# A transformer block on one core: part of the first modulation row moved to VectorE, ScalarE and GpSimd, four early loads into rooms of later tiles, and the last norm's rows left in PSUM

## Chip, core and metric

The kernel runs on one core of one Trainium2 chip. The metric is device time in microseconds (us); the median of three runs of the kernel before is 1842.34 us (1841.93 to 1842.74).

## What is computed

One block on 256 tokens of width 2048, in float32. A condition vector `c` gives six modulation rows of 2048 (shift, scale and gate, for each half of the block); the first half mixes tokens by windowed attention and by a gated delta rule, the second is a mixture of 32 experts, of which each token takes two:

```python
mod = (silu(c) @ w_ada + b_ada)[:, None, :]            # 2048 x 12288
sh1, sc1, g1, sh2, sc2, g2 = split(mod, 6)
u = layer_norm(x) * (1 + sc1) + sh1
mix = token_mixer(u, w_in, ...)                         # u @ w_in, attention, delta rule, w_out
x = layer_norm(ALPHA * x + g1 * mix, ln1_g, ln1_b)
u = layer_norm(x) * (1 + sc2) + sh2
ffn = hier_moe(u, ..., w_gate_up, w_down)
x = layer_norm(ALPHA * x + g2 * ffn, ln2_g, ln2_b)      # the result
```

The change touches the way `sh1` is summed, the loads of the weights of `sh1` and `sc1`, a small constant, and the last `layer_norm`.

## The kernel before

Weights come from HBM in tiles of 128x2048 floats (1024 KB). `wload` (L75) takes a buffer from a pool of four and issues the load on SyncE's queue (SP), which works in order: a load whose buffer is still in use holds every load behind it.

`first_mods` (L157) makes `sc1` (`i` = 1) and `sh1` (`i` = 0) in four quarters `q` of 512 columns. For each it loads four tiles and multiplies every one with the replicated silu of `c` on TensorE (L179; a float32 matmul shows as two records, so a tile is eight). ScalarE copies the sum out of PSUM (L186); `use` (L159) sums the four groups of partitions by four small matmuls (L163, eight records) and adds the bias (L164). After the shift of a quarter, `use` also modulates the quarter's four blocks of the normalised, transposed input: VectorE scales and shifts (L168), ScalarE casts to the high part `uh` (L169), VectorE makes the low part `ul` (L170). `use` runs one tile late: the last shift of a quarter is summed after the first tile of the next quarter's scale. `first_mods` is a generator and gives way after each tile.

The first projection is split by the same quarters. `quarter` (L299) lists ten jobs per quarter: half a weight tile is split into a high part on ScalarE (`wh`, L262) and a low part on VectorE (`wl`, L263), with two buffers for `wl`, and multiplied by three matmuls per block (L267 to L269, `wq`). The sum is copied out by ScalarE in the first quarter (L321) and added by VectorE in the others (L323). `run` (L332) goes through the jobs and, four times per job, adds `per / 4` to a counter and takes a step of the given generator when it reaches 1: this writes the order of the work out by hand. Nine steps of `first_mods` come before the jobs; then each of the first three quarters takes up to eight steps of the next quarter's modulation at `QCH` = 0.73 per job (L754).

Later `ada_steps` (L198) makes the other four modulation rows: VectorE multiplies and adds tile by tile (L207), beside the rest of the projections. `gates` (L367) uses a small selection matrix `sel`, reduced from the identity (L378).

The experts run in 16 pairs: `gate_up` (L1166) multiplies 16 tiles, `turned` (L1185) transposes, `down` (L1202) multiplies eight tiles in four column blocks and adds to the residual (L1225 to L1230). Their loads go round `rings` of 17 buffers: four of `wload`, six and seven of two other pools (L1239); the last loads avoid the four of `wload` (L1250), since `last_rows` (L1350) places the gain and bias of the last norm there, each in a tile of 128x2048: TensorE spreads a row over the partitions (L152) into PSUM and ScalarE copies it (L1355), in the last pair. After a branch for overfull experts, the last norm runs on VectorE: `ln_affine` (L126) makes two passes over each of five pieces, which are then written out (L1397 to L1399).

## Time and profile before

| what | before |
|---|---|
| median of three runs | 1842.34 us (1841.93 to 1842.74) |
| the profiled execution | 1841.24 us |
| its span, first to last instruction | 1839.4 us |
| TensorE busy | 1746.7 us, 95% of the span |
| VectorE busy | 904.7 us, 49% |
| ScalarE busy | 516.3 us, 28% |
| GpSimd busy | 42.0 us, 2% |
| HBM traffic | 624.64 MB read, 341 GB/s over the span |
| mean granted TensorE clock | 0.985 |

Busy shares are means over stages with different limits, so a stage is read by itself: its busy times, its DMA rate, and which wait ends last. TensorE's busy time contains matmuls whose ends are modelled. A row of a timeline that stands for several instructions (`x8`) gives the time from the first's start to the last's end.

### The profile page before, as it was taken

The page shows a single profiled execution, that of the slowest core. Times are in us where ns is not written, and L with a number is a line of the kernel's source. Part 1 is how long each engine was busy: PE and PEld are TensorE (multiplying, and loading weights), DVE is VectorE, ACT ScalarE, POOL GpSimd, SP SyncE. Part 2 cuts the span into 40 slices and gives each one's busy share as a digit, 9 for nine tenths or more (in the row PEclk, how much of TensorE's full clock was granted, in tenths as well). Part 3 has the DMA queues.
Part 4 walks back from the last instruction along what each step waited for, and adds up shares of the span by engine and source line. Part 5 has one row for each costly group of instructions (what it writes and reads, how often), then busy time and mean ns, then how long its engine had stood idle before and what let it go on. Part 6 is the DMA issues. An engine that isn't in the chain of part 4 may idle for free. (4 is left out here: it accounts for less than half of the span.)

```text
span 1839.4 us, 27526 instructions
## 1 busy us (share of the span) xinstructions
PE 1746.7 (95%) x11546; PEld 1126.4 (61%) x11546; DVE 904.7 (49%) x1440; ACT 516.3 (28%) x956; POOL 42.0 (2%) x47
## 2 busy tenths in 40 slices
PE   5999999999999999998999999999999999999995
PEld 2778988898999999986444443444434444343431
DVE  3355898788878878668233212332223312232125
ACT  2433699336333444434211100111001111011111
POOL 1000000102000000000000000000000000000000
PEclk8999999999999999999999999999999999999998
DMA  8887666555877578878899999999999999999994
GB/s 351 318 326 292 227 232 229 182 207 190 300 267 275 201 285 325 345 303 348 327 380 421 420 420 421 420 420 420 421 421 420 420 420 421 420 420 422 420 420 193
DMA packets 87287, 628.57 MB, mean 342 GB/s; under 512 B 9828, under 2 KB 9828, under 8 KB 11252
## 3 DMA queue, kind: packets, MB, share of 16 engines
q1 hardware_dynamic: 86832, 626.42, 85.5%
q8 instruction: 92, 1.51, 0.3%
q10 hardware_dynamic: 328, 0.36, 0.1%
q14 instruction: 35, 0.29, 0.0%
HBM read 624.64 MB, written 2.10 MB: 341 GB/s over the span
## 5 line engine op out<-in xcount | busy, mean ns | idle before, releaser
L262 ACT CAST wh<-w 128x1024 fp32r<-128x1024 f32 x216 | 225.8, 1049 | 312.8 <-PE ws L268 109.5
L263 DVE TENSOR_TENSOR wl<-w,wh 128x1024 fp32r<-128x1024 f32 x216 | 264.8, 1226 | 84.9 <-PE mx L268 22.8
L1175 PE MATMUL pg<-w,XT 128*64 128x512 f32 x1024 | 278.3, 599 | 4.0 <-DMA w<-in_w_gu 3.6
L1175 PE MATMUL pu<-w,XT 128*64 128x512 f32 x1024 | 274.7, 592 | 0.0
L267 PE MATMUL ws<-uh,wh 128*128 128x256 f32 x896 | 261.5, 292 | 1.1 <-ACT wh L262 1.1
L269 PE MATMUL ws<-uh,wl 128*128 128x256 f32 x896 | 254.5, 284 | 4.2 <-DVE wl L263 3.8
L268 PE MATMUL ws<-ul,wh 128*128 128x256 f32 x896 | 253.8, 283 | 0.0
L1213 PE MATMUL pd<-w,hT 128*64 128x512 f32 x1016 | 234.3, 600 | 0.8 <-DVE hT L1190 0.8
L1182 DVE TENSOR_TENSOR hs<-hs,pu 128x512 f32<-128x512 f32 x16 | 11.0, 688 | 431.4 <-PE pu L1175 431.4
L267 PEld LDWEIGHTS ws<-uh,wh 128*128 128x128 f32 x896 | 170.0, 190 | 11.6 <-issue 7.5
L269 PEld LDWEIGHTS ws<-uh,wl 128*128 128x128 f32 x896 | 170.1, 190 | 8.1 <-DVE wl L263 6.5
L268 PEld LDWEIGHTS ws<-ul,wh 128*128 128x128 f32 x896 | 170.2, 190 | 0.5 <-issue 0.5
L207 DVE SCALAR_TENSOR_TENSOR acc<-w,csil,acc 128x1024 f32<-128x1024 f32 x128 | 164.0, 1297 | 10.4 <-DMA w<-in_w_ada 10.3
L1175 PEld LDWEIGHTS pu<-w,XT 128*64 128x64 f32 x1024 | 77.5, 137 | 146.4 <-issue 146.4
L1175 PEld LDWEIGHTS pg<-w,XT 128*64 128x64 f32 x1024 | 72.3, 137 | 134.9 <-issue 112.1
L1154 PEld LDWEIGHTS xg<-G,xh 128*128 128x128 f32 x1024 | 121.0, 195 | 40.5 <-issue 25.0
L1213 PEld LDWEIGHTS pd<-w,hT 128*64 128x64 f32 x1016 | 66.4, 136 | 123.7 <-issue 109.3
L1154 PE MATMUL xg<-G,xh 128*128 128x128 f32 x1024 | 132.6, 284 | 6.5 <-DVE x L1230 3.8
L1181 ACT ACTIVATE hs<-pg 128x512 f32<-128x512 f32 x16 | 9.6, 597 | 453.3 <-PE pg L1175 453.3
L357 ACT CAST dh<-pd 128x512 fp32r<-128x512 f32 x64 | 37.5, 585 | 281.7 <-DVE pd L1216 160.7
L1216 DVE SCALAR_TENSOR_TENSOR pd<-pd,wsl,g2b 128x512 f32<-128x512 f32 x64 | 48.5, 758 | 104.6 <-PE pd L1213 104.6
L267 PE MATMUL wq<-uh,wh 128*128 128x256 f32 x320 | 91.5, 289 | 5.1 <-ACT wh L262 2.8
(362 smaller groups left out, 2300.7 us busy)
## 6 DMA issues: line engine op xcount, KB each, us to landing
w<-in_w_gu SPq DMA_DIRECT2D x256, 1024.0 KB, 19.8
w<-in_w_dn SPq DMA_DIRECT2D x127, 1024.0 KB, 19.8
w<-in_w_ada SPq DMA_DIRECT2D x64, 1024.0 KB, 5.2
w<-in_w_in SPq DMA_DIRECT2D x56, 1024.0 KB, 4.9
w<-in_w_a SPq DMA_DIRECT2D x32, 1024.0 KB, 7.1
w<-in_w_kq SPq DMA_DIRECT2D x20, 1024.0 KB, 6.6
w<-in_w_pab SPq DMA_DIRECT2D x16, 1024.0 KB, 5.5
w<-in_w_out SPq DMA_DIRECT2D x16, 1024.0 KB, 5.8
```

Of the source, the lines that this page charges most:

```text
L207: V.scalar_tensor_tensor(acc[:, hc], w[:, hc], csil[:, k:k + 1], acc[:, hc], op0=MUL, op1=ADD)
L262: SC.copy(h, w)
L263: V.tensor_tensor(lo, w, h.bitcast(F32), op=SUB)
L267: T.matmul(p, a[0], b[0], start=first, stop=False)
L268: T.matmul(p, a[0], b[1], start=False, stop=False)
L269: T.matmul(p, a[1], b[0], start=False, stop=last)
L357: SC.copy(h, src)
L1154: T.matmul(p[:, k * P:(k + 1) * P], xh[t][:, (4 * kq + k) * P:(4 * kq + k + 1) * P], Gs[t].bitcast(F32), start=(t == 0), stop=(t == NT - 1))
L1175: T.matmul(dst[64 * e:64 * e + 64, :], XT[:, k, 64 * e:64 * e + 64], we[:, e * 1024 + hv * 512:e * 1024 + hv * 512 + 512], start=(k == 0), ...
L1182: V.tensor_tensor(hs, hs, pup, op=MUL)
L1213: T.matmul(pd[64 * e:64 * e + 64, :], hT[:, f, 64 * e:64 * e + 64], we[:, (2 * (f % 2) + e) * 512:(2 * (f % 2) + e + 1) * 512], start=(f = ...
L1216: V.scalar_tensor_tensor(pd, pd, ws, g2b[:, cs], op0=MUL, op1=MUL)
```

## The change

`first_mods` is rewritten. The scale's four quarters and the shift's first stay on TensorE (`on_pe`), but are turned by four transposes and a reduce on VectorE, and the first shift is used at once. The other three quarters of the shift go to `beside`: VectorE multiplies and adds two of the four tiles, ScalarE multiplies the other two, GpSimd adds those up, and four small matmuls sum the partitions. The first four weight tiles go to rooms of tiles that are used later (the delta rule's `G1`, and `X1`); two of the four tiles of each shift quarter go to a room of their own beside the accumulators. The steps per quarter become ten, at 1.15 per job. `sel` becomes a loaded constant. The last norm's rows are spread after the branch into eight PSUM banks and read there, in 512-column passes with eight output transfers; the last expert loads keep their usual buffers.

```diff
-QCH = 0.73
+QCH = 1.15
-LT = (0, 0)
...
+    def early_room():
+        a = r1.tile([P, 1024 + 7 * 512], F32, tag="G1", name="wx0")
+        b = r2.tile([P, KT, S], F32, tag="X1", name="wx1").rearrange("p k s -> p (k s)")
+        return [t[:, 2048 * j:2048 * j + 2048] for t in (a, b) for j in range(2)]
...
+        def turn(i, q, mr):
+            dst, b = column(i, q)
             p = pg(f"fc{i}{q}")
             for m in range(4):
-                T.matmul(p[:, m:m + 1], mr[:, m * P:(m + 1) * P], C("s4"), start=True, stop=True)
+                T.transpose(p[:, m * P:(m + 1) * P], mr[:, m * P:(m + 1) * P], ident)
+            V.tensor_reduce(dst, p.rearrange("p (m j r) -> p m j r", m=4, j=4)[:, :, :, 0], axis=AX.X, op=ADD)
+            V.scalar_tensor_tensor(dst, dst, float(i), b, op0=ADD, op1=ADD)
...
+        def load(i, q, t):
+            src = A["w_a01"][(4 * i + q) * 4 + t]
+            if room:
+                w = room.pop(0)
+                nc.sync.dma_start(w, src)
+                return w
+            return wload(src)
+
+        def on_pe(i, q):
+            pa = pg(f"fa{i}{q}")
+            for t in range(4):
+                w = load(i, q, t)
+                for k in range(4):
+                    T.matmul(pa[32 * k:32 * k + 32, :], crep[:, 4 * t + k, :], w[:, 512 * k:512 * k + 512],
+                             start=(t == 0), stop=(t == 3))
+                if t < 3:
+                    yield
+            mr = rb.tile([P, 512], F32, tag="mr", name=f"fr{i}{q}")
+            SC.copy(mr, pa)
+            turn(i, q, mr)
+            yield
+
+        def beside(q, acc, own):
+            for t in range(4):
+                if t % 2:
+                    w = load(0, q, t)
+                else:
+                    w = own
+                    nc.sync.dma_start(w, A["w_a01"][4 * q + t])
+                for k in range(4):
+                    wk, ck = w[:, 512 * k:512 * k + 512], csil[:, 4 * t + k:4 * t + k + 1]
+                    if t % 2 == 0:
+                        if t == k == 0:
+                            V.tensor_scalar(acc[0], wk, ck, None, op0=MUL)
+                        else:
+                            V.scalar_tensor_tensor(acc[0], wk, ck, acc[0], op0=MUL, op1=ADD)
+                    elif t == 1 and k == 0:
+                        SC.activation(acc[1], wk, AF.Copy, scale=ck)
+                    else:
+                        tmp = acc[2 + k % 2]
+                        SC.activation(tmp, wk, AF.Copy, scale=ck)
+                        G.tensor_tensor(acc[1], acc[1], tmp, op=ADD)
+                    if k % 2:
                         yield
+            G.tensor_tensor(acc[0], acc[0], acc[1], op=ADD)
+            yield
+            dst, b = column(0, q)
+            p = pg(f"fs{q}")
+            for m in range(4):
+                T.matmul(p[:, m:m + 1], acc[0][:, m * P:(m + 1) * P], ones[:, 0:1], start=True, stop=True)
+            V.tensor_tensor(dst, p[:, 0:4], b, op=ADD)
+
+        yield from on_pe(1, 0)
+        yield from on_pe(0, 0)
+        modulate(0)
+        yield
+        ms = r1.tile([P, 1024 + 7 * 512], F32, tag="G1", name="ms")
+        acc = [ms[:, 512 * j:512 * j + 512] for j in range(4)]
+        for q in range(1, 4):
+            side, main = beside(q, acc, ms[:, 2048:4096]), on_pe(1, q)
+            for n in range(9):
+                next(side, None)
+                if n < 4:
+                    next(main)
                 yield
+            next(side, None)
+            modulate(q)
+            yield
...
-        sel = gd.tile([P, 16], F32, name="sel")
-        V.tensor_reduce(sel, ident.rearrange("p (j c) -> p c j", j=4)[:, :16, :], axis=AX.X, op=ADD)
+        sel = M("sel")
...
-        run(few(mods, 8), QCH, split_at=2 * TQ)
+        run(few(mods, 10), QCH, split_at=2 * TQ)
...
-        if nld[0] > 12 * NE - len(AHEAD) - 8 and ring is wload:
-            ring = 1
...
-        if pr == NP - 1:
-            l2g, l2b = last_rows(8), last_rows(12)
...
+    l2 = []
+    for j in range(8):
+        p = (ps_gu, ps_gu, ps_d, ps_m)[j // 2].tile([P, 512], F32, tag="gudm"[j // 2], name=f"l2{j}")
+        spread(p, rows, 8 + j)
+        l2.append(p)
...
-    for t, c0, c1 in ((0, 0, 1024), (0, 1024, D), (1, 0, 1024), (1, 1024, 1536), (1, 1536, D)):
-        ln_affine(x[t], x[t], mv[:, t, 0:1], rs[:, t], l2g, l2b, slice(c0, c1))
-        nc.sync.dma_start(out[t * P:(t + 1) * P, c0:c1], x[t][:, c0:c1])
+    chunks = [(t, c, slice(c * 512, (c + 1) * 512)) for c in range(4) for t in range(NT)]
+    for t, c, cs in chunks[:2]:
+        V.scalar_tensor_tensor(x[t][:, cs], x[t][:, cs], mv[:, t, 0:1], l2[c], op0=SUB, op1=MUL)
+    for t in range(NT):
+        V.reciprocal(rs[:, t], rs[:, t])
+    for t, c, cs in chunks[2:]:
+        V.scalar_tensor_tensor(x[t][:, cs], x[t][:, cs], mv[:, t, 0:1], l2[c], op0=SUB, op1=MUL)
+    for t, c, cs in chunks:
+        V.scalar_tensor_tensor(x[t][:, cs], x[t][:, cs], rs[:, t], l2[4 + c], op0=MUL, op1=ADD)
+        nc.sync.dma_start(out[t * P:(t + 1) * P, cs], x[t][:, cs])
```

## Rows read from the trace of the kernel before

**Rows 1.** Busy time by stretch: start:end, length, then busy time and instructions of TensorE (PE), its weight loads (PEld), VectorE (DVE), ScalarE (ACT) and GpSimd (POOL), granted TensorE clock, busy share of the DMA engines, GB/s. The second quarter of the first projection, and a part of the expert phase.

```profile
85.00:126.00 41.00, 39.83 (x320) 32.14 (x320) 21.36 (x31) 12.90 (x16) 0.00 (x0) 1.00 0.89 337
...
1100.00:1400.00 300.00, 293.14 (x1449) 124.32 (x1447) 84.99 (x170) 30.90 (x67) 0.00 (x0) 1.00 1.01 420
```

**Rows 2.** Timeline of TensorE over the start: start, length, engine, line, operation, output and inputs, records, and in brackets the idle time before it with what ended it. The last modulation tiles, the eight small matmuls that sum up the shift, and the first product of the projection.

```profile
28.68 1.06 PE L179 MATMUL fa<-w,crep 128*32 128x512 f32 x8 [1.22 <-DMA w<-in_w_a]
...
32.59 1.93 PE L179 MATMUL fa<-w,crep 128*32 128x512 f32 x8 [2.84 <-DMA w<-in_w_a]
...
35.18 1.94 PE L179 MATMUL fa<-w,crep 128*32 128x512 f32 x8 [0.67 <-DMA w<-in_w_a]
...
37.05 1.87 PE L163 MATMUL fc<-cst,fr 128*128 128x1 f32 x8
...
41.72 0.58 PE L267 MATMUL wq<-uh,wh 128*128 128x256 f32 x1 [2.81 <-ACT wh L262]
```

**Rows 3.** Timeline of SyncE's queue over the start: loads of modulation tiles, the sixth and seventh in one row, then the eighth.

```profile
18.85 5.31 SPq L77 DMA_DIRECT2D w<-in_w_a  x2
...
24.69 0.33 SPq L77 DMA_DIRECT2D w<-in_w_a  x1
```

**Rows 4.** Busy time by stretch, columns as in rows 1, at the start.

```profile
22.50:25.00 2.50, 2.50 (x27) 0.71 (x25) 0.00 (x0) 1.47 (x4) 0.00 (x0) 1.00 0.46 147
...
25.00:27.50 2.50, 2.46 (x24) 1.13 (x16) 0.16 (x1) 0.28 (x1) 0.00 (x0) 1.00 0.81 318
...
32.50:35.00 2.50, 1.93 (x8) 0.20 (x8) 0.00 (x0) 0.35 (x1) 0.00 (x0) 0.50 1.03 436
```

**Rows 5.** Timeline of VectorE over the start: its first operation on data, and the add that makes the first quarter's shift.

```profile
9.19 0.26 DVE L378 TENSOR_REDUCE sel<-cst 128x16 f32<-128x64 f32 x1 [9.08 <-DMA cst<-in_cst]
...
38.95 0.16 DVE L164 SCALAR_TENSOR_TENSOR sh1c<-fc,craw 128x4 f32<-128x4 f32 x1 [12.29 <-PE fc L163]
```

**Rows 6.** Timeline of TensorE around the beginning of the second quarter (three rows), and the first product of the third.

```profile
81.53 1.93 PE L179 MATMUL fa<-w,crep 128*32 128x512 f32 x16
...
83.38 1.05 PE L163 MATMUL fc<-cst,fr 128*128 128x1 f32 x8
...
85.58 0.50 PE L267 MATMUL wq<-uh,wh 128*128 128x256 f32 x2 [1.14 <-ACT uh L169]
...
126.58 0.50 PE L267 MATMUL wq<-uh,wh 128*128 128x256 f32 x2 [1.14 <-ACT uh L169]
```

**Rows 7.** Groups of instructions from 1740 us to the end, forms kept apart: line, engine, operation, tiles, shapes, count, then busy time in us and mean ns of one, and idle time before. The norm's second pass on 512 columns, a VectorE pass with PSUM, a ScalarE copy of 512 columns, and the spread rows on TensorE.

```profile
L128 DVE SCALAR_TENSOR_TENSOR x<-x,rsd,l 128x512 f32<-128x512 f32 x2 | 1.5, 749 | 0.0
...
L1216 DVE SCALAR_TENSOR_TENSOR pd<-pd,wsl,g2b 128x512 f32<-128x512 f32 x8 | 6.0, 754 | 10.9 <-PE pd L1213 10.9
...
L1355 ACT COPY l<-l 128x512 f32<-128x512 f32 x8 | 4.6, 586 | 17.2 <-PE l L152 9.2 <-DMA w<-in_w_gu 8.0
...
L152 PE MATMUL l<-rows,cst 16*128 16x512 f32 x16 | 8.4, 626 | 0.3 <-DVE x L1230 0.3
```

**Rows 8.** Groups of instructions of GpSimd over the whole span, columns as in rows 7: two kinds of 128x512 passes.

```profile
L596 POOL TENSOR_TENSOR G<-G,dec 128x512 f32<-128x512 f32 x4 | 4.2, 1041 | 128.2 <-DVE G L577 64.2 <-PE qs L580 64.0
...
L620 POOL TENSOR_TENSOR o<-o,ssq 128x512 f32<-128x512 f32 x4 | 6.1, 1543 | 49.7 <-DVE ssq L618 49.7
```

**Rows 9.** Timeline of VectorE in a later stage, where GpSimd works beside it: the same two operations without and with a GpSimd pass over them.

```profile
316.67 1.28 DVE L207 SCALAR_TENSOR_TENSOR acc<-w,csil,acc 128x1024 f32<-128x1024 f32 x1
...
318.57 0.15 DVE L482 TENSOR_TENSOR wj<-rn 128x8 f32<-128x8 f32 x1
...
320.48 1.26 DVE L484 TENSOR_TENSOR wk<-wj,kdw 128x8 f32<-128x8 f32 x1
...
324.05 2.06 DVE L207 SCALAR_TENSOR_TENSOR acc<-w,csil,acc 128x1024 f32<-128x1024 f32 x1
```

**Rows 10.** Timeline of GpSimd in the same stretch.

```profile
319.40 2.32 POOL L507 TENSOR_TENSOR G<-G,cmx 128x512 f32<-128x512 f32 x1 [71.22 <-issue]
...
322.80 2.22 POOL L486 TENSOR_TENSOR G<-G,wk 128x512 f32<-128x512 f32 x2
```

**Rows 11.** Timeline of TensorE in the expert phase: the last matmul that waits for a weight tile, the last down matmuls, and the last matmul of all.

```profile
1732.97 1.08 PE L1175 MATMUL pg<-w,XT 128*64 128x512 f32 x4 [0.56 <-DMA w<-in_w_gu]
...
1818.47 1.08 PE L1213 MATMUL pd<-wl,hT 128*64 128x512 f32 x4
...
1821.87 0.73 PE L1226 MATMUL cb<-dl,GT 128*128 128x512 f32 x2
```

**Rows 12.** Waits of SyncE's queue from 1700 us on: who waited for whom, us in total, times, longest.

```profile
SPq L1273 <- PE pd L1213: 3.8, 1, 3.8
```

**Rows 13.** Busy time by stretch, columns as in rows 1, near the end.

```profile
1810.00:1812.00 2.00, 2.00 (x9) 0.47 (x5) 1.29 (x3) 0.58 (x1) 0.00 (x0) 1.00 0.51 207
...
1824.00:1826.00 2.00, 0.00 (x0) 0.00 (x0) 1.73 (x5) 0.48 (x2) 0.00 (x0) 0.95 0.01 4
```

**Rows 14.** Timelines of VectorE (two rows) and of SyncE's queue at the end: begin and last pass of the last norm, and the output transfers.

```profile
1825.17 0.39 DVE L1393 BATCH_NORM_AGGREGATE mvd<-sd 128x2 f32<-128x24 f32 x2 [0.27 <-DVEq L1386]
...
1834.88 0.75 DVE L128 SCALAR_TENSOR_TENSOR x<-x,rsd,l 128x512 f32<-128x512 f32 x1
...
1829.30 6.69 SPq L1399 DMA_DIRECT2D out<-x  x5
```

**Rows 15.** DMA issues of the page (part 6): tile, engine, operation, count, KB each, median us from issue to landing.

```profile
w<-in_w_a SPq DMA_DIRECT2D x32, 1024.0 KB, 7.1
```

More of the change, by code (lines that the diff above doesn't have):

```diff
@@ L155, in ada_tile, with column @@
         return wload(A["w_ada"][k * P:(k + 1) * P, (i - 2) * D:(i - 1) * D])
+    def early_room():
+        a = r1.tile([P, 1024 + 7 * 512], F32, tag="G1", name="wx0")
+        b = r2.tile([P, KT, S], F32, tag="X1", name="wx1").rearrange("p k s -> p (k s)")
+        return [t[:, 2048 * j:2048 * j + 2048] for t in (a, b) for j in range(2)]
     def first_mods():
-        def use(i, q, mr):
-            dst = (sh1c, sc1c)[i]
+        def column(i, q):
+            return (sh1c, sc1c)[i][:, 4 * q:4 * q + 4], craw[:, KT * (i + 1) + 4 * q:KT * (i + 1) + 4 * q + 4]
+        def turn(i, q, mr):
+            dst, b = column(i, q)
@@ L172, in first_mods @@
-        late = []
-        for q in range(4):
-            for i in (1, 0):
-                pa = pg(f"fa{i}{q}")
-                for t in range(4):
-                    w = wload(A["w_a01"][(4 * i + q) * 4 + t])
-                    for k in range(4):
-                        T.matmul(pa[32 * k:32 * k + 32, :], crep[:, 4 * t + k, :], w[:, 512 * k:512 * k + 512],
-                                 start=(t == 0), stop=(t == 3))
-                    if late and t == LT[1 - i]:
-                        use(*late.pop())
-                    if t < 3:
-                        yield
-                mr = rb.tile([P, 512], F32, tag="mr", name=f"fr{i}{q}")
-                SC.copy(mr, pa)
-                if i == 0 and LT[0] < 0:
-                    use(i, q, mr)
-                else:
-                    late.append((i, q, mr))
+                T.transpose(p[:, m * P:(m + 1) * P], mr[:, m * P:(m + 1) * P], ident)
@@ new lines, in turn, with modulate @@
+            V.tensor_reduce(dst, p.rearrange("p (m j r) -> p m j r", m=4, j=4)[:, :, :, 0], axis=AX.X, op=ADD)
+            V.scalar_tensor_tensor(dst, dst, float(i), b, op0=ADD, op1=ADD)
+        def modulate(q):
+            for k in range(4 * q, 4 * q + 4):
+                V.tensor_scalar(xT[:, k, :], xT[:, k, :], sc1c[:, k:k + 1], sh1c[:, k:k + 1], op0=MUL, op1=ADD)
+                SC.copy(uh[:, k, :], xT[:, k, :])
+                V.tensor_tensor(ul[:, k, :], xT[:, k, :], uh[:, k, :].bitcast(F32), op=SUB)
@@ new lines, in first_mods @@
+        room = early_room()
+        def load(i, q, t):
[18 more added lines that the diff above has]
+            yield
@@ L191, in first_mods @@
+        yield from on_pe(1, 0)
[10 more added lines that the diff above has]
+                    next(main)
                 yield
-        if late:
-            use(*late.pop())
@@ L748, in tile_block @@
     dsts = [a0[:, i:i + 2, :] for i in range(11)] + [None] + [szT[:, i:i + 2, :] for i in range(7)] + [None]
-    for _ in range(8 - FM + (LT[0] >= 0)):
+    for _ in range(9 - FM):
         next(mods)
@@ L1348, in overflow @@
                 V.bn_stats(sd[:, t, c, :], x[t][:, c * 512:(c + 1) * 512])
-    def last_rows(q):
-        l2 = wp.tile([P, D], F32, tag="w", name=f"l2{q}")
-        for c in range(4):
-            p = pm(f"l2{q + c}")
-            spread(p, rows, q + c)
-            SC.copy(l2[:, c * 512:(c + 1) * 512], p)
-        return l2
     for pr in range(NP):
```

19 lines of the change are left out of this document (3 added, 16 removed).

## The prediction, made before the changed kernel ran

> **What bounds the kernel now.** I read the span by stages first. In a quarter of the first projection TensorE is busy 39.83 of 41 us while the DMA moves 337 GB/s; in the expert phase the DMA moves 420 GB/s for hundreds of us, its ceiling here [rows 1]. So the early stage is set by TensorE, the late one by the weight stream, and time saved early is handed on: the later weight loads are queued when earlier tiles come free, not at a fixed time. The chain of waits that ended last shows only the last norm on VectorE; it does not reach back, so the three places of the change are read one by one.
>
> Start: the first quarter cannot begin before eight weight tiles are multiplied. TensorE waits for the seventh and eighth, then runs the next quarter's first tile, and only then sums up the shift [rows 2]. The loads were late, not slow: with four buffers the queue issued the sixth at 18.85, the seventh at the end of that row (23.83) and the eighth at 24.69 us, as buffers came free [rows 3], and the DMA fell to 147 and 318 GB/s between full stretches [rows 4].
>
> Quarters: from one first matmul to the next is 41.0 us (85.58 to 126.58). At the boundary come two tiles of modulation products, eight small matmuls, and 1.14 us of idle time for the modulated rows [rows 6].
>
> End: TensorE last waits for a weight tile at 1732.97 us; after that it is behind the stream [rows 11]. In the last expert pair it also spreads eight rows, 8.4 us of it [rows 7]. The last tile's load waited 3.8 us for a buffer that TensorE held [rows 12], and the stream was already ebbing at 1810 to 1812 [rows 13], yet the last down matmuls end at 1818.47 + 1.08 = 1819.55. So the end waits for TensorE, not for bytes.
>
> **The change, part by part.**
>
> *Early rooms.* Four loads move ahead of the SP waits; the queue's order is kept, and all eight tiles are in flight before a buffer is awaited. The gap that closes is 2.5 x (420 - 147)/420 + 2.5 x (420 - 318)/420 = 2.2 us [rows 4]. The eighth was matched with its matmul at 32.59; queues share bandwidth with the load behind, so I take 3.4 us earlier, between 2.2 (the gap alone) and 4.4 (strict order of bytes): 29.2. Its eight records take 1.93, since the granted clock is 0.50 there, the 1.2 GHz level, after idle time [rows 2, 4]; I keep that, as TensorE will again wait between tiles. Then, without the next tile in between: copy 0.6 [rows 7], four transposes at half of the eight small matmuls' 1.87, so 0.9 [rows 2], a reduce and an add, 0.4 with hand-overs 0.8. Before, the add began at 38.95 [rows 5] and the first product at 41.72 [rows 2]: 2.8 later. New: 29.2 + 1.9 + 0.6 + 0.9 + 0.8 + 2.8 = 36.2. **Gain 5.5**, bounds 4.3 and 6.7. The removed reduce held VectorE until 9.45 [rows 5]; what then runs earlier still waits for tiles, so nothing; its result becomes 16 constant columns, 8 KB beside tiles of 1024 KB, nothing either. The memsets that shared a room with the new tiles leave the start; attention needs them only after the quarters, and GpSimd is otherwise empty there: nothing.
>
> *Three quarters of the first shift off TensorE.* Four tiles per quarter leave it: two cost 83.38 - 81.53 = 1.85 [rows 6], so 3.7. Of two sets of eight small matmuls (1.05 each) one becomes four transposes, 0.5 saved; the other stays. The modulation is queued over a job before the quarter ends, so the 1.14 us can hide. That is 5.3 us at most.
> VectorE gets eight 128x512 products of 0.75 [rows 7], 6.0 on top of 21.36 [rows 1]: 27.4. ScalarE gets eight of 0.59 [rows 7], 4.7 on top of 12.90: idle enough. GpSimd gets eight additions of 1.04 to 1.54 [rows 8], 8 to 12 us: room enough. ScalarE now waits for GpSimd through two scratch tiles, with its next casts behind; at two products per step, a step every three us or so, 2 x 1.04 fits. VectorE waits for its own weight tile with the next low half behind it; that tile is ahead of the next projection tile in the same queue, so no wait is added while the stream is ahead. The stream carries the same thirteen tiles: 13 x 1.05 MB at 420 GB/s is 32.5 us, below what remains.
> What eats into it is GpSimd beside VectorE. During a GpSimd pass over 512 elements, a 128x8 VectorE operation took 1.26 instead of 0.15 and a 128x1024 one 2.06 instead of 1.28 [rows 9, 10]: 0.8 to 1.1 us lost for one that is caught. About every second addition should catch one: 8 x 0.5 = 4 us, VectorE at 31.4 of some 37. It has slack except near the boundary, where the modulation, an evacuation and the next low half stand in one row. I charge 1.3 us per quarter there. **Gain 5.3 - 1.3 = 4.0 per quarter, 12 for three**; bounds 5.3 x 3 = 16 and, if VectorE binds, 1.
> The Trainium skill, SBUF — State Buffer, section Who interferes with whom, says that GpSimd reads and VectorE instructions with two SBUF inputs exclude each other for a whole instruction. The trace agrees that VectorE is held [rows 9]; taken to the letter, with all eight additions blocking for 1.04, VectorE would have 35.7 us of work in a quarter and the gain would be some 3 us each.
>
> *The last norm's rows.* Eight spreads and eight copies leave the last pair, and the last loads keep their usual buffers, so the last tile's load is not held up. TensorE could come 8.4 us earlier; the bytes allow about as much (last landing near 1810 plus one tile's 1.08, against 1819.55). TensorE then meets tiles as they land, one per 2.5 us, and loses part: I take 7.2. The spreads come back after the branch: TensorE is free from 1822.60 [rows 11], VectorE's norm starts at 1825.17 [rows 14], and each spread is 8.4/8 = 1.05, so the first two rows stand before they are wanted and the last at some 1822.9 + 8.4 = 1831.3, where VectorE reaches the second half at about 1830.5 and needs its fourth row 3 us later. No wait if the clock stays at its upper level. VectorE's 16 passes of at most 0.75, with PSUM too [rows 7], are 12.0 if nothing of one lies under the next, against 1825.17 to 1835.63 now for the same columns; the chunks are independent, so I take no change and 1.5 as the bound. Eight output transfers, 2.1 MB, now leave within some 5 us instead of the 6.7 of the five [rows 14], at the ceiling of 420 GB/s, so I let the last land 0.5 later. **Gain 6.7**; bounds 9 and -3 (no lag won, spreads exposed).
>
> **Sum.** 5.5 + 12 + 6.7 = 24.2 us. The profiled execution took 1841.24 us for a span of 1839.4, 1.1 below the median 1842.34. 1842.34 - 24.2 = **1818.1**.
>
> **Rivals.**
> 1. *VectorE becomes the bound of the quarters.* For: rows 9. If each addition takes 1.54 [rows 8] and holds it throughout, it has 27.4 + 12.3 = 39.7 us of work, 0.4 per quarter saved with no idle time at all: 5.5 + 1 + 6.7 = 13, **1829**. Against: four GpSimd passes took 1.04 [rows 8], and VectorE's evacuations take one operand from PSUM. By the Trainium skill's rule above alone (SBUF — State Buffer, Who interferes with whom) it would lie at 1821. Chance 0.15.
> 2. *The end gives nothing back.* TensorE's lag is not the spreads', or they run after the branch at the lower clock (granted 0.95 at 1824 to 1826, once TensorE was idle [rows 13]) and double to 16.8 us, so that the beta rows are late by several us: 5.5 + 12 = 17.5, **1825**. Against: TensorE is busy to 1822.60, just before. Chance 0.12.
> 3. *Slower: VectorE waits for its own tile.* If SP reaches the two own loads of a quarter only when VectorE already stands at them, each costs a whole flight, 7.1 us as the median of such loads now [rows 15], and the low half, the evacuation and TensorE stand behind it: 2 x 7.1 x 3 = 42.6 less the 24.2, **1861**. It decides where the loss passes 8 us per quarter. Against: SP ran several tiles ahead in every quarter, and the own tile's buffer is free a third of a quarter earlier. Chance 0.04.
> 4. *The rooms do not do what they say*: the eighth tile lands no earlier, since bandwidth is shared with later loads. Then the start gives only the dropped tile, 2 us: **1822**. Chance 0.07.
>
> **Numbers.** Forecast 0.62, rivals as above. The range goes down to the upper bounds of two terms beside the expected end or start, 6.7 + 16 + 9 = 31.7, so 1810, and up past rivals 2 and 4 to rival 1, 1830. Its edges leave out rival 3, and mishaps added up. A difference under 0.2% (3.7 us) a measurement of this kernel can hardly tell from none. Faster 0.94, within 0.02, slower 0.04.
>
> **What would show it.** The eighth tile's matmuls near 29 and the first product near 36 us; first products of the quarters 37 us apart, with no TensorE wait for the modulated rows; VectorE passes stretched to 1.5 to 2 us beside GpSimd; in the last pair no gap between landing and use, the last down matmuls ending some 7 us closer to the stream's end; the eight spreads done before VectorE wants them. Wrong would be quarters still 40 us apart, TensorE waiting for the low half or a weight tile for several us per quarter, or VectorE waiting for a spread.

## The result: slower, 1854.67 us

| | before | after |
|---|---|---|
| median | 1842.13 us (1841.33 to 1842.74) | 1854.67 us (1852.51 to 1855.92) |
| profiled execution, span | 1841.24, 1839.4 us | 1855.92, 1854.0 us |
| first product of quarter 1 of the first projection | 41.72 us | 35.45 us |
| of quarters 2, 3, 4 | 85.58, 126.58, 167.71 us | 89.70, 133.44, 177.95 us |
| last matmuls of the down stage (L1213, now L1265) end | 1819.55 us | 1828.05 us |
| last norm, begin and end | 1825.17 to 1835.63 us | 1833.65 to 1850.05 us |

The ratio of the times is 1.0063, 95% interval 1.0050 to 1.0076. Slower had been given a chance of 0.04, and the time lies outside the range. In what follows a run's distance from the kernel before is its ratio, from executions of both on one chip, times 1842 us.

**The start came as forecast.** TensorE's timeline, to be held against [rows 2]:

```profile
29.27 1.93 PE L193 MATMUL fa<-w,crep 128*32 128x512 f32 x8 [1.41 <-DMA w<-in_w_a]
...
31.96 1.11 PE L168 MATMUL fc<-cst,fr 128*128 128x128 f32 x4 [0.77 <-ACT fr L198]
...
35.45 0.58 PE L320 MATMUL wq<-uh,wh 128*128 128x256 f32 x1 [2.37 <-ACT wh L315]
```

The eighth tile is multiplied at 29.27 (forecast 29.2), the projection begins 6.3 us earlier (forecast 5.5). This is one profile against one. In the four profiles whose start is that of before (before, x2, x7, x11 of the experiments) the first product lies at 41.20 to 43.66, in the fourteen with the new start at 34.04 to 35.73: the means are 7.7 us apart. A quarter, too, can differ by more than a microsecond between executions: the second took 41.0 us in before and x2, and 42.3 in x7 and x11, with the same code up to there.

**The quarters grew.** From 35.45 to 89.70 is 54.2 us, then 43.7 and 44.5, where before had 43.9, 41.0 and 41.1 and the forecast was 37 for the later ones. After's waits from 8 to 185 us (who waited for whom, us in total, times, longest):

```profile
ACT ms L220 <- POOL ms L221: 12.1, 8, 1.9
...
PE wq L320 <- ACT wh L315: 10.2, 10, 2.4
PE fs L229 <- POOL ms L224: 8.0, 3, 2.7
```

GpSimd stands at the end of two of the three: ScalarE waits for GpSimd (the two scratch tiles), and once per quarter TensorE waits for GpSimd itself. TensorE's wait for ScalarE's casts is mostly not GpSimd's: in x12, the same front without GpSimd's additions, it is still 7.8 us. The timeline of all engines ahead of the first of those three waits, in order of start:

```profile
71.28 1.34 ACT L220 ACTIVATE ms<-w,csil 128x512 f32<-128x512 f32 x2
...
72.14 5.95 POOL L221 TENSOR_TENSOR ms<-ms 128x512 f32<-128x512 f32 x4 [11.54 <-ACT ms L220]
...
74.01 0.73 ACT L220 ACTIVATE ms<-w,csil 128x512 f32<-128x512 f32 x1 [1.40 <-POOL ms L221]
...
76.02 1.98 ACT L315 CAST wh<-w 128x1024 fp32r<-128x1024 f32 x2
...
77.09 4.29 DVE L316 TENSOR_TENSOR wl<-w,wh 128x1024 fp32r<-128x1024 f32 x2 [4.26 <-ACT wh L315]
...
78.17 2.12 POOL L224 TENSOR_TENSOR ms<-ms 128x512 f32<-128x512 f32 x1
...
80.35 1.87 PE L229 MATMUL fs<-cst,ms 128*128 128x1 f32 x8 [2.74 <-POOL ms L224]
```

GpSimd had been idle for 11.54 us; then the quarter's last four additions come at once, 1.49 us each, and a final one of 2.12. Two low halves beside them take 4.29 us, where 1.22 each is usual. After TensorE's wait its matmuls run at the lower clock (columns as in [rows 1]):

```profile
72.00:80.00 8.00, 5.61 (x46) 5.31 (x45) 3.74 (x3) 5.88 (x9) 7.54 (x5) 1.00 0.91 303
80.00:90.00 10.00, 9.65 (x57) 9.65 (x58) 6.66 (x14) 3.01 (x7) 0.29 (x1) 0.66 0.44 152
...
168.00:178.00 10.00, 9.59 (x55) 9.59 (x56) 6.39 (x12) 3.15 (x7) 3.24 (x10) 0.66 0.44 154
```

The granted clock is 0.66 in the ten microseconds around the end of the wait at 80.35, and again around the one at 168.41: some 6.8 us of each ran at 0.50, the 1.2 GHz level, with TensorE's idle time of 2.6 to 2.7 us at its beginning. The DMA falls from 303 to 152 GB/s there. In the waits of SyncE's queue over the same stretch, a load waits for a buffer with ScalarE's products in it:

```profile
SPq L76 <- ACT ms L220: 11.7, 6, 5.0
```

GpSimd's groups over the quarters show what the additions cost:

```profile
L221 POOL TENSOR_TENSOR ms<-ms 128x512 f32<-128x512 f32 x21 | 33.0, 1569 | 125.5 <-ACT ms L220 124.3
L224 POOL TENSOR_TENSOR ms<-ms 128x512 f32<-128x512 f32 x3 | 6.4, 2125 | 0.2
```

**The end.** The delay of 10.2 us at the fourth quarter has grown to 12.7 when the loads of `w_out` begin (759.31 against 746.59) and stands at 12.74 when SyncE's queue issues the last pair's loads (1748.23 against 1735.49): the stream hands a delay on like a lead. The last down matmuls are late by 8.5 alone, so the last pair gained 4.2. The norm then lost 5.9. The chain of waits that ended last (start, length, what):

```profile
1834.57 0.04 issue
1834.62 14.00 PE l L147 x16
1848.62 0.03 issue
1848.64 0.75 DVE x L1448
```

The timeline of all engines in the same stretch, to be held against [rows 14]:

```profile
1834.62 13.99 PE L147 MATMUL l<-rows,cst 16*128 16x512 f32 x16 [3.51 <-PEq L1426]
1836.70 1.41 DVE L1442 SCALAR_TENSOR_TENSOR x<-x,mvd,l 128x512 f32<-128x512 f32 x2 [2.07 <-PE l L147]
1838.40 1.40 DVE L1446 SCALAR_TENSOR_TENSOR x<-x,mvd,l 128x512 f32<-128x512 f32 x2 [0.30 <-PE l L147]
...
1844.30 6.11 SPq L1449 DMA_DIRECT2D out<-x  x8
...
1848.64 1.41 DVE L1448 SCALAR_TENSOR_TENSOR x<-x,rsd,l 128x512 f32<-128x512 f32 x2 [0.30 <-PE l L147]
```

The busy times there, columns as in [rows 1]:

```profile
1835.00:1840.00 5.00, 5.00 (x7) 1.87 (x7) 2.81 (x4) 0.00 (x0) 0.00 (x0) 0.50 0.00 0
1840.00:1845.00 5.00, 5.00 (x8) 1.87 (x7) 4.21 (x6) 0.00 (x0) 0.00 (x0) 0.50 0.00 2
```

TensorE comes out of the branch 3.51 us late ("PEq" is its sequencer), VectorE after 0.26. The sixteen records then run at a granted clock of 0.50, the 1.2 GHz level, 14.0 us where [rows 7] has 8.4, and VectorE waits 0.30 for every row.

The sum on the profiled spans: 12.74 late in the stream, less 4.2, plus 5.9 in the norm, plus 0.2 for the tail behind the last pass: 14.6 = 1854.0 - 1839.4.

### The profile page after: what moved, and what is told of

Same layout as the page of the kernel before. It is cut to its first block, busy times and chain, and to the rows that moved or that the text cites. A ratio compares the mean times of both kernels' runs of the same rounds, so it can differ in the third digit from the quotient of the medians.

```text
span 1854.0 us, 27407 instructions
## 1 busy us (share of the span) xinstructions
PE 1747.6 (94%) x11430; PEld 1131.4 (61%) x11430; DVE 931.6 (50%) x1474; ACT 525.1 (28%) x969; POOL 83.0 (4%) x71
## 3 DMA queue, kind: packets, MB, share of 16 engines
q8 instruction: 91, 1.49, 0.3%
## 5 line engine op out<-in xcount | busy, mean ns | idle before, releaser
L316 DVE TENSOR_TENSOR wl<-w,wh 128x1024 fp32r<-128x1024 f32 x216 | 271.6, 1261 | 91.3 <-ACT wh L315 36.7
L1265 PE MATMUL pd<-w,hT 128*64 128x512 f32 x1016 | 234.3, 600 | 0.8 <-DVE hT L1242 0.8
L1206 PEld LDWEIGHTS xg<-G,xh 128*128 128x128 f32 x1024 | 118.9, 192 | 40.8 <-issue 25.0
L1265 PEld LDWEIGHTS pd<-w,hT 128*64 128x64 f32 x1016 | 66.5, 136 | 123.6 <-issue 109.1
L410 ACT CAST dh<-pd 128x512 fp32r<-128x512 f32 x64 | 37.5, 585 | 281.7 <-DVE pd L1268 160.4
L320 PE MATMUL wq<-uh,wh 128*128 128x256 f32 x320 | 96.6, 302 | 11.5 <-ACT wh L315 10.2
```

The costliest lines, as they stand in the source:

```text
L316: V.tensor_tensor(lo, w, h.bitcast(F32), op=SUB)
L320: T.matmul(p, a[0], b[0], start=first, stop=False)
L410: SC.copy(h, src)
L1206: T.matmul(p[:, k * P:(k + 1) * P], xh[t][:, (4 * kq + k) * P:(4 * kq + k + 1) * P], Gs[t].bitcast(F32), start=(t == 0), stop=(t == NT - 1))
L1265: T.matmul(pd[64 * e:64 * e + 64, :], hT[:, f, 64 * e:64 * e + 64], we[:, (2 * (f % 2) + e) * 512:(2 * (f % 2) + e + 1) * 512], start=(f = ...
```

## The experiments

Sixteen kernels. The time of each is its median, then its ratio to before with the interval. x5, x9, x12 and x14 leave out part of the shift's sum, so they measure what a part costs and are no candidates themselves.

**x1 to x4: which part, and the first theories.** x1 is the change with the end of before; x2 is before with the change's end; x3 has the early rooms and the first shift used at once, with all products on TensorE.

```diff
 x3, against x1:
-        for q in range(1, 4):
-            side, main = beside(q, acc, ms[:, 2048:4096]), on_pe(1, q)
-            ...
+        for q in range(1, 4):
+            yield from on_pe(1, q)
+            yield from on_pe(0, q)
+            modulate(q)
+            yield
 (9 steps per quarter at QCH = 1.0)
 x4, against x1: the odd tiles of the shift in rooms of their own
-                    w = load(0, q, t)
+                    w = two[t // 2]
+                    nc.sync.dma_start(w, A["w_a01"][4 * q + t])
+        x2 = r2.tile([P, NT, D], F32, tag="X2", name="wx2")
+        two = [x2[:, j, :] for j in range(2)]
```

> The whole first part of the change, with the end of the kernel before (rows copied to SBUF in the last pair, two passes over five pieces). In the changed kernel the last pair's loads were issued 12.7 us later than before (1748.23 against 1735.49), so if the first part alone makes that delay: 1842.1 + 12.7 = 1855, 1852 to 1857. If the delay came with the end's different buffers, 1842 or less.

> Only the last norm's part of the change, on the kernel before. Theory: leaving the spreads out of the last pair gives TensorE 4.2 us back (as 12.7 late became 8.5 late between the loads and the last down matmuls of the changed kernel), and the spreads behind the branch cost 5.9 at the lower clock, so 1842.1 + 1.9 = 1844, 1842 to 1846. Rival, the prediction's own term: 6.7 faster, 1835.4.

> Early rooms and the first shift used at once, but all quarters of the shift on TensorE as before, no products on VectorE, ScalarE or GpSimd; end of before. If the start's 6.3 us are kept and only the moved products cost time: 1842.1 - 6.3 = 1836, 1833 to 1837. If the faster start is itself what the buffers pay back in the first quarter: 1841 to 1843.

> As the first part alone, but the two tiles of each shift quarter that ScalarE reads get a room each of their own (in the room of the input, which is free by then), so that the pool of four buffers holds only projection and scale tiles. Theory one, the ring of four buffers taken in strict order and held by ScalarE's tiles for 20 us: the first quarter falls from 54 to about 42 us and the others to 40, so 1842.1 - 10 = 1832, 1828 to 1838. Theory two, GpSimd holding VectorE and the sums waiting for GpSimd: nearly nothing changes, 1850 to 1856.

Measured: x1 1851.76 (1.0049, 1.0033 to 1.0066), +9.0 us; x2 1846.06 (1.0022, 1.0012 to 1.0032), +4.1; x3 1839.51 (0.9988, 0.9978 to 0.9998), -2.2; x4 1846.81 (1.0028, 1.0016 to 1.0041), +5.2. Both halves lose by themselves and their sum, 13.1, is the change's 11.6 within the intervals. x1 lies just under the range expected of it, x2 just above its own. The rooms work at the start, but x3 missed its 1833 to 1837 us: its first product comes at 34.08, and then its second and third quarters take 43.6 and 43.7 us where before took 41.0 and 41.1, so that 3.8 us of the lead are left at the fourth. All its products are on TensorE, so neither GpSimd nor the moved products can be the reason; which other part of the new order costs this was not tried. x4 fell between the two theories: the pool held by ScalarE's tiles is some 4 us of the front's loss, give or take as much, and not most.

**x5, x6, x9, x12: GpSimd, ScalarE, the pool.**

```diff
 x5, against x4 (x12 is the same edit on x1):
-                        G.tensor_tensor(acc[1], acc[1], tmp, op=ADD)
-            G.tensor_tensor(acc[0], acc[0], acc[1], op=ADD)
 x9, against x5:
-                    elif t == 1 and k == 0:
-                        SC.activation(acc[1], wk, AF.Copy, scale=ck)
-                    else:
-                        tmp = acc[2 + k % 2]
-                        SC.activation(tmp, wk, AF.Copy, scale=ck)
 x6, against x4:
-        for q in range(1, 4):
+        yield from on_pe(1, 1)
+        yield from on_pe(0, 1)
+        modulate(1)
+        yield
+        for q in range(2, 4):
 (9 steps at QCH = 1.0 in the first quarter)
```

> The own rooms of x4 for the odd shift tiles, the end as before, and GpSimd's additions left out (the shift's columns of three quarters are then VectorE's half of the products alone: ScalarE's products are made and not added). x4 took 1846.8 us, 4.7 above before. Theory GpSimd: each of three quarters loses 2.7 us in TensorE's wait for the sum and more in stretched low halves (1456 ns of one against 1221) and in the lower clock behind the wait; without GpSimd that is gone: 1840 us (1837 to 1843), first projection products of the second and third quarter about 38.5 us apart where x4 has 40.0 and 41.0. Rival, ScalarE's order: the loss is in the first quarter, where TensorE waits 8.8 us for ScalarE's high halves because copies out of PSUM and products stand in front of them: the first quarter stays at 50 us or more of x4's 51.7, and the time at 1844 to 1847.

> As x4, but the shift's products that fall into the first quarter are left on TensorE; those of the second and third stay on VectorE, ScalarE and GpSimd. Rival, ScalarE's order: the first quarter is then as long as with the rooms alone (42.6 us, x4 has 51.7), the others as in x4 (40.0 and 41.0): 1838 us (1835 to 1841). Theory GpSimd: one of three waits for the sum is spared and what it costs, some 3 us: 1844 us (1842 to 1846), the first quarter 48 us.

> x5 with ScalarE's products left out as well (half of the shift's terms of three quarters are then missing; the tiles are still loaded). x5 took 1834.4, its first quarter 46.8 us and the next two 38.6 and 38.7. Theory ScalarE's order: what is left of the first quarter's loss is ScalarE's, whose copies out of PSUM, casts and products stand in one queue: the first quarter falls to 42 to 43 us (as with the rooms alone) and the time to 1830.5 (1828 to 1833). Rival: ScalarE has room for products and the first quarter is long for another reason (VectorE's products before the low halves, the copies): the first quarter stays above 46, the time at 1833 to 1836.

> x1 (the change's front, the end as before) with GpSimd's additions left out; ScalarE's tiles still come through the pool of four buffers. x1 took 1851.8. With own rooms the additions cost 12.4 us (x4 to x5) and the pool 5.0 (x1 to x4). If the two are separate: 1839.4 us (1837 to 1842). If the pool's buffers were held because ScalarE waited for GpSimd: no more than with own rooms, 1834.5 (1832 to 1837).

Measured: x5 1834.44 (0.9948, 0.9932 to 0.9965), -9.6 us; x12 1833.33 (0.9948, 0.9931 to 0.9965), -9.6; x9 1835.22 (0.9954, 0.9937 to 0.9970), -8.5; x6 1839.82 (0.9979, 0.9967 to 0.9990), -3.9. Without GpSimd's additions the pool makes no difference (x5, x12), so its buffers were held because ScalarE waited for GpSimd. x5 came out below both ranges expected of it; its second and third quarters, 38.6 and 38.7 us, are those of the theory that names GpSimd. ScalarE's products cost nothing that shows (x5, x9), so the theory that they crowd its queue falls; x6 met that theory's number, with the first quarter at 42.7 us, but it also takes a third of GpSimd's work away, and that is the likelier reason. In x6 the two quarters that kept GpSimd took 42.7 and 42.9 us, not x4's 40.0 and 41.0; why is open. In x12 the first products of the second, third and fourth quarter lie 37.5 and 37.4 us apart:

```profile
80.09 0.28 PE L322 MATMUL wq<-uh,wh 128*128 128x256 f32 x1
...
117.57 0.28 PE L322 MATMUL wq<-uh,wh 128*128 128x256 f32 x1
...
154.95 0.28 PE L322 MATMUL wq<-uh,wh 128*128 128x256 f32 x1
```

**x13, x14: the three ways in which GpSimd costs.** From x1 to x12 are 18.6 us.

```diff
 x13, against x1: eight scratch tiles for two
-                        tmp = acc[2 + k % 2]
+                        tmp = many[4 * (t // 2) + k]
 x14, against x13:
-            G.tensor_tensor(acc[0], acc[0], acc[1], op=ADD)
```

> x1 (the change's front, the end as before), but each of ScalarE's eight products of a quarter has a scratch tile of its own, so that ScalarE waits for GpSimd no more; the additions and the sum that TensorE waits for stay. x1 took 1851.8, without additions (x12) 1833.3. If most of the 18.5 us come from ScalarE standing behind GpSimd, with the casts behind it and the pool's buffers held: 1840 us (1837 to 1843), and no wait of ScalarE for GpSimd. If they come from TensorE's wait for the sum and the clock behind it, or from VectorE being held: 1848 to 1852.

> As x13, and the last addition of a quarter is left out, so that TensorE's small products take VectorE's half alone (the other half of the terms is then missing): GpSimd's seven additions a quarter run beside VectorE as before, and nobody waits for them. If GpSimd's holding of VectorE is most of the 18.5 us: 1845 us or more, low halves stretched as in x1. If it is the waits: 1834 to 1837. x13 less this run is the wait for the sum: by the profile 3 times 2.7 us and the clock, some 8 to 10.

Measured: x13 1847.62 (1.0025, 1.0015 to 1.0035), +4.6 us; x14 1841.14 (0.9997, 0.9984 to 1.0009), -0.6. So the three share the loss: ScalarE's wait 9.0 - 4.6 = 4.4, the wait for the sum 4.6 + 0.6 = 5.2, and GpSimd running beside VectorE with nobody waiting for it 9.6 - 0.6 = 9.0; each is uncertain by 3 to 4 us, as the intervals show, and each holds for this order of taking things away. In x13's profile TensorE waits for the sum only once, 3.7 us. Both clean expectations, all waits or all holding, fell. The low halves and the modulation's passes in x14, then in x12, from 34 to 165 us (groups as in [rows 7]):

```profile
L321 DVE TENSOR_TENSOR wl<-w,wh 128x1024 fp32r<-128x1024 f32 x32 | 44.9, 1423 | 16.3 <-ACT wh L320 15.4 <-PE wq L327 0.8
...
L178 DVE TENSOR_SCALAR xT<-xT,sc1c,sh1c 128x256 f32<-128x256 f32 x13 | 10.4, 847 | 0.1
```

```profile
L318 DVE TENSOR_TENSOR wl<-w,wh 128x1024 fp32r<-128x1024 f32 x35 | 42.0, 1219 | 15.3 <-ACT wh L317 13.4 <-PE wq L324 1.9
...
L178 DVE TENSOR_SCALAR xT<-xT,sc1c,sh1c 128x256 f32<-128x256 f32 x16 | 5.9, 422 | 0.2
```

With the same waits taken away, a low half takes 1423 against 1219 ns in the mean and a modulation pass 847 against 422, and the later quarters take 40.8 and 40.7 us in x14 against 37.5 and 37.4. Read one by one, the low halves that meet no addition take 1.22 us in both; in x14 six of 39 take 2.29 to 2.33. The additions of the change take 1.27 to 1.30 us where they meet no VectorE work, and the eight longest, which stand beside low halves, 2.12 to 2.36. Two things limit what x14 says of the change. The modulation's passes are caught because nobody waits for the sum there; in the change they come after it and take 408 ns. And the granted clock differs too (columns as in [rows 1]; two stretches of x14, then the second and third quarter of x12):

```profile
109.40:112.80 3.40, 3.14 (x15) 3.15 (x15) 3.36 (x4) 0.00 (x0) 3.32 (x2) 0.50 1.02 422
150.30:153.70 3.40, 3.40 (x19) 3.40 (x18) 3.36 (x4) 0.41 (x1) 3.24 (x3) 0.50 1.03 416
```

```profile
80.09:117.57 37.48, 35.45 (x286) 30.87 (x285) 25.39 (x38) 17.65 (x24) 0.00 (x0) 1.00 0.91 364
117.57:154.95 37.38, 35.41 (x286) 30.88 (x285) 25.92 (x38) 18.80 (x25) 2.92 (x9) 1.00 0.92 365
```

x5, which has no additions either, has two stretches at 0.50 like those of x14 (107.1 to 110.5 and 144.6 to 148.0) and quarters of 38.6, so of the 3.3 us between x14 and x12 some 1.2 may belong to the clock alone.

**x7, x8, x11: the end.**

```diff
 x7, against before (x8: the same on x3):
-        if nld[0] > 12 * NE - len(AHEAD) - 8 and ring is wload:
+        if nld[0] > 12 * NE - len(AHEAD) - 3 and ring is wload:
 x11, against x2:
-    mxc = nc.values_load(cmax[0:1, 0:1], min_val=0, max_val=S)
-    with tc.If(mxc > CAP):
-        overflow()
```

> The kernel before with one number changed: its two held tiles of norm rows stay, but only the last two loads, not the last eight, are kept from the pool that they are held in. If the 4.2 us that the change wins back in the last pair come from loads that wait for the other pool's buffers, most of them come back here with the norm as before: 1838.5 us (1837.5 to 1840). If they come from the spreads themselves leaving TensorE (eight matmuls with their copies, 3 to 4 us in the last pair), this stays at 1842 (1841 to 1843).

> x3 (early rooms, the first shift used at once, all products on TensorE) and x7's end together. x3 took 1839.5, 2.5 below before. If the shift of the start is handed on through all stages and the end's gain is a thing of its own, the two add: 1836 us (1834 to 1838). If the end's gain isn't there: 1839.5 (1838 to 1841).

> x2 (before's front, the change's end), with the branch that this data never takes left out, the load of its condition too. x2 took 1846.1. If the end's loss is the wait of 3.5 us behind the branch and the spreads at the lower clock (0.87 us each against 0.53 in the last pair): the spreads start right behind the last down products at the upper clock, and the norm is VectorE's own: 1836 us (1834 to 1839). If sixteen spreads on the path cost as much without the branch (lower clock all the same): 1842 us (1840 to 1844).

Measured: x7 1842.78 (0.9998, 0.9989 to 1.0008), x8 1839.26 (0.9982, 0.9973 to 0.9992), -3.3 us and within its interval of x3. The edit reaches fewer loads than eight: by the traces, four of the last pair's loads go to the held pool in the change and in x2, none in before, and two in x7. The last load is then issued 62.1 us after the pair's first, where before took 68.1, and yet from the pair's first load to the last down matmul it is 84.07 us in x7 and 84.06 in before, against 79.81 in the change. Nothing is won by the earlier load; what is left for the 4.2 us that the last pair gained is TensorE's own time for the spreads. x11 1841.64 (0.9987, 0.9975 to 0.9998), 6.4 us better than x2. Its last norm:

```profile
1823.94 4.14 PE L148 MATMUL l<-rows,cst 16*128 16x512 f32 x6
...
1826.52 1.39 DVE L1381 SCALAR_TENSOR_TENSOR x<-x,mvd,l 128x512 f32<-128x512 f32 x2
1827.82 0.22 DVE L1383 RECIPROCAL rsd<-rsd 128x1 f32<-128x1 f32 x2
1827.95 4.02 DVE L1385 SCALAR_TENSOR_TENSOR x<-x,mvd,l 128x512 f32<-128x512 f32 x6
1831.89 5.35 DVE L1387 SCALAR_TENSOR_TENSOR x<-x,rsd,l 128x512 f32<-128x512 f32 x8
```

No pass waits for a row any more, and the sixteen passes take 10.7 us in a piece, as the prediction had them. But the other ten records ran earlier, from 1766.66 on, in TensorE's time in the last pair; so x11 gives up 2.7 of the 4.2 us again (82.55 us for the same stretch). Its number lies in the range of the second theory, sixteen spreads on the path at the lower clock, but not for that reason: no spread is on the path. The six records here took 0.69 us each, the granted clock falling from 1.00 to 0.50 between 1822 and 1828: without the branch the lower clock comes too, but while VectorE is busy with earlier rows.

**x10, x15, x16: the version that the runs point to.** All sixteen products of a quarter on VectorE, none on ScalarE or GpSimd, the end as before.

```diff
 x15, against x1 (x10: the same on x4):
-                    if t % 2 == 0:
-                        ...
-                        G.tensor_tensor(acc[1], acc[1], tmp, op=ADD)
+                    if t == k == 0:
+                        V.tensor_scalar(acc[0], wk, ck, None, op0=MUL)
+                    else:
+                        V.scalar_tensor_tensor(acc[0], wk, ck, acc[0], op0=MUL, op1=ADD)
-            G.tensor_tensor(acc[0], acc[0], acc[1], op=ADD)
 x16, against x15:
                 if q == 0:
-                    SC.copy(dst, p)
+                    V.tensor_copy(dst, p)
```

> The own rooms of x4, and all sixteen products of a quarter on VectorE: nothing on ScalarE or GpSimd, nothing left out. Eight more products of about 0.61 us make 4.9 us a quarter of VectorE, which was busy 26.7 us of 38.6 in x5's second quarter: 31.6. If VectorE beside no GpSimd has that room: 1834 us (1831 to 1838). Rival, VectorE's order: the low halves queue behind eight more products, TensorE waits for them some 2 to 3 us a quarter and the clock falls: 1842 us (1839 to 1846).

> x12's tiles (the pool of four buffers for the odd ones), and all sixteen products of a quarter on VectorE, none on ScalarE or GpSimd, nothing left out. With own rooms (x10) this took 1838.4, and the pool made no difference without GpSimd (x5 to x12). VectorE's 4.9 us more a quarter against x12's 1833.3: 1836.5 us (1834 to 1839), which would beat both kernels. If VectorE now holds the pool's buffers, since its products stand behind low halves: 1842 us (1840 to 1846).

> x15 with one line changed: in the first quarter the ten copies out of PSUM are made by VectorE instead of ScalarE. x15's first quarter is 47.8 us, with all products on TensorE (x3) it was 42.6; VectorE's extra passes cost 0.7 us each. If ScalarE's order is what keeps the first quarter long (a copy that waits for TensorE stands in front of the next casts, so that TensorE then waits for these): the first quarter falls to 44 us or less and the time to 1834 (1832 to 1836). If the first quarter is VectorE's or the stream's: 47 us or more, and 1837 to 1841.

Measured: x10 1838.40 (0.9976, 0.9966 to 0.9986), x15 1837.29 (0.9976, 0.9964 to 0.9987), -4.4 us each; x16 1836.00 (0.9958, 0.9945 to 0.9972), -7.7. x10 fell between its two theories, x15 met its first, x16 reached the edge of its first. x16 beats both kernels. Its first quarter fell from x15's 47.8 to 44.0 us, and TensorE's wait for high halves with it. Waits in x15's first quarter, 34 to 82 us:

```profile
PE wq L316 <- ACT wh L311: 7.6, 7, 2.4
```

And in x16's, 34 to 79 us:

```profile
ACT wh L311 <- DMA w<-in_w_kq: 18.8, 4, 9.2
...
PE wq L316 <- ACT wh L311: 2.4, 1, 2.4
```

So a copy out of PSUM that waits for TensorE, with the next casts behind it on ScalarE, kept x15's first quarter long. Not all of the 3.8 us need be its own: the granted clock is 0.86 in x15's first quarter and 0.91 in x16's. What ScalarE then waits for most is the stream: 18.8 us for weight tiles, while the DMA moves 368 GB/s. The gain in time from x15 to x16 is within the two intervals.

## Why the prediction was wrong, step by step

*Early rooms: right, and rather more than forecast.* 6.3 us for 5.5 in the two profiles; the means of all profiles are 7.7 apart, above the upper bound of 6.7 (by its own terms 5.5 + 4.4 - 3.4 = 6.5). x3 shows the part alone (first product at 34.08). It does not show that the whole lead is handed on: x3's time is 2.2 us shorter.

*TensorE's saving per quarter: there, but smaller.* x12's quarters of 37.5 and 37.4 us look like the forecast "37 us apart". That forecast had 1.3 us for GpSimd taken off, though, and x12 has no additions: to be held against its 3.6 us are the 5.3 before the charge. x5, with own rooms, saves 2.4. With all sixteen products on VectorE (x15) the quarters take 39.6 and 38.9 us.

*The step that failed: "GpSimd gets eight additions of 1.04 to 1.54, 8 to 12 us: room enough", and with it "a step every three us or so, 2 x 1.04 fits".* Room in the sum is not room in time. The additions took 1.57 us each and 2.13 for the last, and they do not come evenly: four products stand together before the boundary, so that four additions and the final one are a chain of 8.2 to 9.6 us in front of the sum. ScalarE's two scratch tiles turned that into waits of ScalarE and the pool (4.4 us by x1 and x13), TensorE's wait for the sum brought 2.7 us a quarter and the lower clock (5.2 us by x13 and x14), where the prediction let ScalarE's wait fit and had no wait for the sum.

*The charge for GpSimd beside VectorE: mis-sized.* It was 1.3 us a quarter; x14 against x12 gives 3.3 in the later quarters, 9.0 us over all, with the reservations made there. The prediction took it that VectorE has slack except near the boundary; but TensorE's waits for low halves grow (5.3 us in x14, 1.2 in x12, from 34 to 165 us), and ScalarE's waits for the modulation with them (10.2 against 4.6).

The Trainium skill (SBUF — State Buffer, section Who interferes with whom) says that a VectorE instruction with two SBUF inputs and a GpSimd instruction that reads SBUF exclude each other for a whole instruction, and that the issue order decides who blocks. The runs agree in both directions: a low half of 1.22 us takes up to 2.33 beside additions (1423 ns in the mean of x14, 1513 of x13), and an addition of 1.27 to 1.30 us up to 2.36 beside low halves (1569 ns in the mean of the change). The 1041 ns of [rows 8] are another operation's; no addition of these runs was below 1.26 us. By the letter of the rule the quarter's gain would have been 3 us; x14's 40.7 us, against 41.0 before, left 0.3.

*The first quarter: a saving that was not there.* Forecast 39.9 us, in x12 44.4, before 43.9. The three quarters were taken as alike, but only in the first does ScalarE copy the sums out of PSUM, and with the new order of steps such a copy stands in front of the casts: TensorE's wait for high halves in this quarter is 6.9 us in x12 and 2.8 in before. The copies alone do not do it: x3, with the same copies and all products on TensorE, has 2.5. x16 shows this cause for the version with all products on VectorE; x12 with the copies moved was not run, and x16's own 44.0 us are not 39.9 either.

*A lead is handed on: right up to a part.* x12 leads by 12.8 us at the fourth quarter, by 8.8 at 472 us and by 10.1 from 692 us on, up to the stream, and its span ends 7.6 shorter. The fall from 11.6 to 8.8 comes at 449.4 to 456.2 us, where x12's granted clock is 0.50. In x5 and x4 a like part goes in stretches where the granted clock is below before's (0.73 at 215 to 225 us in x5, 1.00 before). What lowers it there was not tried.

*The last pair: mis-sized.* Of 7.2 us forecast came 4.2. TensorE then does meet tiles as they land, as the prediction said, one per 2.49 us, up to 1805:

```profile
1802.96 1.08 PE L1227 MATMUL pg<-w,XT 128*64 128x512 f32 x4 [0.55 <-DMA w<-in_w_gu]
1805.45 1.08 PE L1227 MATMUL pg<-w,XT 128*64 128x512 f32 x4 [0.55 <-DMA w<-in_w_gu]
```

Held buffers were no part of it (x7).

*The spreads behind the branch: the second step that failed.* "TensorE is free from 1822.60" was read from its last matmul, and a branch that VectorE passes in 0.27 us was taken to be passed by TensorE as well; it cost 3.51 us (4.01 in x2). The trace of before had this already. There the branch occupies TensorE's sequencer for 3.3 us from 1822.5 on, to 1825.8, and VectorE's for 0.07 (instructions of the branch's line in before: durations in ns, least, median and most, then first and last start; PEldq is TensorE's sequencer too):

```profile
L1386 PEldq COMPARE_BRANCH  x1: 3335/3335/3335, 1822.5 to 1822.5; - x1
L1386 DVEq COMPARE_BRANCH  x1: 72/72/72, 1824.4 to 1824.4; - x1
```

"No wait if the clock stays at its upper level" named the condition, and it did not hold: rival 2's mechanism, priced at 16.8 us, took 14.0. The norm went from 10.5 to 16.4 us. The Trainium skill (Runtime: NRT & Kernel Launch, section Instruction fetch mechanics) says that a taken branch to a target outside the instruction window stalls until the target has been fetched. That would fit a long skipped branch on TensorE; no run here shows code loading.

**The bill.** The front was to give 17.5 and lost 9.0 (x1), 26.5 us off. GpSimd's additions are 18.6 of it; of the 7.9 left, x12's profile places 7.4 up to 692 us: 4.5 in the first quarter (44.4 for 39.9), 0.7 in the two others, 2.7 lost later, less 0.5 won at the start. The same profile loses 2.5 more up to its end, which the medians do not show (its span is 7.6 us shorter than before's, the ratio gives 9.6). The end was to give 6.7 and lost 4.1 (x2), 10.8 off: 3.0 in the last pair, 6.4 in the norm by x2's own profile, and 1.4 left over, well within x2's interval of 2.2 to 5.9 us.

The rivals: 1 had the right engine pair and 11 of the 18.6 us (its own figures, 39.7 us of VectorE in a quarter of 41.0, would leave a saving of 1.3 and not 0.4); 2 was right about the lower clock behind the branch, but let the end lose nothing by it; 3, the only slower one, looked at VectorE's own tile, for which no wait of note appears. What was missing is a slower rival with GpSimd on the path: a chain of 8 to 10 us in front of each sum, three times.

## What to carry to other kernels

An engine that is idle in the sum of a stage can still be the last link before its boundary: lay the last few operations of the stage out in time, with the longer durations, and see who stands behind them on each queue. Work given to GpSimd beside a VectorE that feeds TensorE was paid for twice here, in its own duration and in VectorE's, and VectorE did the same sums faster alone. What is moved behind a branch starts when the engine that does it has passed the branch: look that engine's own branch up in the trace, and the granted clock behind it.

## What the hardware showed beyond expectation

- A branch that is not entered cost TensorE 3.5 to 4.0 us of idle time (after, x2), and VectorE 0.26. The branch alone took 3.34 us on TensorE's sequencer in before, 3.35 in after and 3.85 in x2; on ScalarE 0.05.
- Over the sixteen spread records behind the branch the granted clock was 0.50 for all 14 us; TensorE had been idle for 3.51 us before them and is shown busy for 5.00 of 5 us in them.
- GpSimd and VectorE slowed each other: 1.28 us alone and up to 2.36 together for a GpSimd addition, 1.22 and up to 2.33 for a low half. A modulation pass, which reads one tile, took 0.41 us alone and 1.18 to 1.46 beside an addition (x14).
